# Folding the first channel mixer as well, with unread products in its pairs

## The chip, the cores and the metric

The kernel runs on one core of a Trainium2 chip. The metric is the device time of one execution in microseconds (us); lower is better. A run of the kernel is timed several times and the median is taken. The profile is one execution more, recorded by the hardware profiler.

## The reference

The reference is a decoder trunk of two layers over one sequence: T = 512 positions, D = 1024 channels, all in float32. Each layer is a token mixer and then a channel mixer, each behind an RMS norm that is modulated by a vector c (adaLN). Layer 0 has a retention as its token mixer, layer 1 an mLSTM. The channel mixer is the same in both layers:

```python
def conv_ffn(h, w_up, conv_w, conv_b, w_down):
    u = causal_dwconv(h @ w_up, conv_w, conv_b)
    a, b = jnp.split(u, 2, axis=-1)
    return (jax.nn.silu(a) * b) @ w_down

def reference(x, c, positions, ...):
    c_act = jax.nn.silu(c)
    for i in range(DEPTH):
        mod = c_act @ ada_w[i] + ada_b[i]
        sh_t, sc_t, gt_t, sh_f, sc_f, gt_f = [m[:, None, :] for m in jnp.split(mod, 6, axis=-1)]
        h = rmsnorm(x, norm_tok_g[i]) * (1.0 + sc_t) + sh_t
        ...
        x = x + gt_t * y
        h = rmsnorm(x, norm_ffn_g[i]) * (1.0 + sc_f) + sh_f
        x = x + gt_f * conv_ffn(h, ffn_w_up[i], ffn_conv_w[i], ffn_conv_b[i], ffn_w_down[i])
    return rmsnorm(x, final_g)
```

The hidden width is 2816, which is 22 tiles of 128 for each of the two halves a and b. "A pair" is the tile f of a and the tile f of b.

## The kernel before

**Products.** Every float32 operand is split into a high part that TensorE takes in one pass and a low part, the rest; a product is three matmuls, high x high, low x high and high x low (mm3, lines 250 to 253). A weight chunk is 128 x 1024 (512 KB): SyncE's queue (SP) loads it into one of 8 raw buffers, ScalarE (ACT) casts the high part (L157, whi) and VectorE (DVE) subtracts for the low part (L162, wlo).

**The program** is a list of items, and an item has the weight chunks that it uses. The loop at its end (lines 1363 to 1371) runs the items in order, and before each item it loads and splits chunks for up to 4 items ahead (class Ahead, line 331), as long as the 8 buffers for split weights allow and no "bar" is passed. `bars` holds the item at which a folded channel mixer starts; no chunk from behind a bar is fetched ahead of it.

**Side gemvs.** The vector c is multiplied with the adaLN weights on DVE: one gemv (line 130) takes a 512 KB load on SP's queue, into the same raw buffers, and one DVE instruction of 1025 elements a partition (L134). Those that aren't wanted at once stand in the list `side`, 80 of them, and one is taken from it after each item that uses weight chunks and is marked free:

```python
        fn([u.chunk for u in uses])
        if uses and free and n > 6 and side:
            side.pop(0)()
```

**The order of the stages** is: retention, channel mixer 0, mLSTM, channel mixer 1, with a seam between each two. At a seam (`boundary`, line 580) the last contraction of a stage is done in two halves of 256 positions, so that the norm of the first half (sums of squares, tile pms; DVE reciprocal; scaling) runs beside the products of the second, and the next stage's first four projections (tile pf, `Start.rest`, line 655) are done in halves too. In the mLSTM the items of `heads` (line 827) stand in this order: projections q, k of heads 0 and 1 with the scores of head 0 after the second projection of head 1, attend of head 0, values of head 1, and so on. The scores (`ml_scores`, line 1270) load two rows from a scratch in DRAM by SP's queue (mb, db), weigh the products with w = exp(...) (L1280 and L1281), and split the result (sp, sl); attend (tile pav) multiplies them with the values.

**Channel mixer 0** is direct: for each pair two projections with products of 512 columns (tile pp, 24 products each), the causal convolution over positions on ACT and DVE, silu and gate; after groups of 6, 8 and 8 tiles come the contractions with w_down (tile po).

**Channel mixer 1** is folded from pair 5 on (`FOLD_FROM`, 17 pairs). `Start.sums` (line 684) and `Start.turn` (line 707) form sums and differences of halves of the input; class Fold (line 183) forms the like of the weights, on DVE, ACT and GpSimd (POOL); seven products of 256 columns take the place of eight (`folded`, line 374; tile p, lines 387 to 389). A pair's products stand in `unit` (line 406) in the order 1, 5, 2, 6, first half of a contraction, 7, second half of it, 4, 3. On TensorE, DVE, ACT and POOL the fold runs in the order written. Its groups are 4, 4, 4, 4 and 6 tiles, and the contractions of the first four stand within the units. Ahead of the fold, items for the pairs 2 to 4 take in the first steps of the fold in pieces (`early`, in `Ffn.items`, line 945).

Of the kernel before, what the change touches and what calls it, by code (L numbers as in the profile page):

```python
# [22 lines left out]
FF = 2816  # L23
FT = FF // P
EPS = 1e-6
GROUPS = [[6, 8, 8], [4, 4, 4, 4, 6]]
WCOLS = 1024
WBUFS = 8
RAWS = 8
FOLD_FROM = 5  # L30
WPAD = 64
OFF = 16
DIRECT = (0, 0)
# [36 lines left out]
def trunk(ctx: ExitStack, tc: tile.TileContext, xT, cb, pos, vec, decay, zmask, ada, w_s0, w_in0, w_v0,  # L70
# [300 lines left out]
            then(ps)  # L371
        item([Use(src, KT * P)], fn)

    def folded(folds, h, terms, pairs, downs, ahead):

        no = lambda *a: None
        banks, sums = {}, {}

        def product(i, n, o, start=False):
            hi, hc, lo, lc = folds[i].p[n]
            for k in range(4):
                b = terms(n, k)
                st, sp = start and k == 0, n in (2, 3, 4) and k == 3
                ch, cl = slice(hc + k * P, hc + k * P + P), slice(lc + k * P, lc + k * P + P)
                PE.matmul(o, hi[:, ch], b[0], start=st, stop=False, skip_group_check=True)  # L387
                PE.matmul(o, hi[:, ch], b[1], start=False, stop=False, skip_group_check=True)  # L388
                PE.matmul(o, lo[:, cl], b[0], start=False, stop=sp, skip_group_check=True)  # L389
# [12 lines left out]
        def last(i):  # L402
            c1, s = banks[i][0], sums[i][0]
            V.tensor_tensor(c1[:, HB], c1[:, HB], s[:, HB], op=ALU.add)

        def unit(i):
            f = folds[i + 1] if i + 1 < len(folds) else None
            d = chunks[i + 1] if i + 1 < len(downs) else None
            with_down = i < len(downs)
            at = pairs[i - 1] if i else None  # L410
            if at:
                last(i - 1)
                at.init(1, banks[i - 1][1])
# [24 lines left out]
            if at:  # L438
                at.silu()
            V.tensor_tensor(c1[:, HA], c1[:, HA], s[:, HA], op=ALU.add)  # L440
            if at:
                at.gate()
            product(i, 6, c2[:, HA])
            A.copy(s[:, HB], c2[:, HA])
            if f:
                f.low_13()
                f.sums_24()
            else:
                ahead.low()
                ahead.low()  # L450
            if at:
                at.high()
                at.low()
            if with_down:
                down(i, 0)
            else:
                product(i, 5, c1[:, HB])
            if f:
                f.high_24()
                f.low_24(i % 2)  # L460
            else:
                ahead.high()
                ahead.high()
            product(i, 7, c2[:, HA])
            A.copy(q[:, HA], c2[:, HA])
            V.tensor_tensor(c2[:, HB], c1[:, HB], q[:, HA], op=ALU.add)
            if d:
                d.high()
                d.low()
            down(i, 1)  # L470
            if f:
                f.high_b()
                f.low_b()
            else:
                ahead.low()
                ahead.low()
            product(i, 4, c2[:, HA])
            product(i, 3, c1[:, HB])
            if i + 2 < len(folds):
                folds[i + 2].load()  # L480
            load_down(i + 2)
            if i == len(folds) - 2:
                for _ in range(4):
                    ahead.load()

# [375 lines left out]
    def gate_col(layer, which):  # L861
        base = (16, 40)[which]
        return lambda m: mods[layer][:, base + m : base + m + 1]


    class Ffn:
        def __init__(self, layer):
            self.layer, self.h, self.gs = layer, [], {}
            t0, t1 = self.pair(0), self.pair(1)
            w = w_up[layer]  # L870
            self.folded = layer == 1
            self.start = Start([w[0], w[FT], w[1], w[FT + 1]], self.h, layer, 1, [t0, t0, t1, t1], self.folded)

        def conv_col(self, f, j):
            return col("fcw", (self.layer * 3 + j) * 2 * FT + f)
# [62 lines left out]
                between()  # L938

        def down(self, gi):  # L940
            base = sum(GROUPS[self.layer][:gi])
            return pieces(lambda i: w_dn[self.layer][gi][i], GROUPS[self.layer][gi], gate_col(self.layer, 1),
                          lambda k: self.gs[base + k])

        def items(self, norm):
            groups = GROUPS[self.layer]
            if self.folded:
                w = w_up[self.layer]
                folds = [Fold((w[f], w[f + FT])) for f in range(FOLD_FROM, FT)]
                pairs = [self.steps(f) for f in range(FOLD_FROM, FT)]  # L950
                downs = [p for gi in range(len(groups) - 1) for p in self.down(gi)]
                steps, run = folded(folds, self.h, self.start.terms, pairs, downs, ahead)

                def early(n):
                    todo = [steps.pop(0) for _ in range(n)]
                    item([], lambda w: [f() for f in todo])
                self.up(2)
                early(1)
                self.up(3, lambda: early(3))
                th = self.pair(4)  # L960
                proj_item(w[4], self.h, th)
                early(len(steps))
                proj_item(w[4 + FT], self.h, lambda ps: (self.start.turn(), th(ps)))
                bars.append(len(items))
                item([], run)
                boundary([], self.down(len(groups) - 1), norm)
                return
            base, nxt = 0, 2
            for gi, n in enumerate(groups):
                upto = base + n + 2 if gi < len(groups) - 2 else FT  # L970
                while nxt < min(upto, FT):
                    self.up(nxt)
                    nxt += 1
                if gi < len(groups) - 1:
                    contract_items(self.down(gi))
                else:
                    boundary([], self.down(gi), norm)
                base += n


    cos, sin = slot("cos"), slot("sin")
# [381 lines left out]
    for n, (uses, fn, free) in enumerate(items):  # L1363
# [112 lines left out]
```

## Time and profile before

| | |
|---|---|
| median of 3 runs | 1569.84 us (1569.71 to 1570.32) |
| the profiled execution, own time | 1570.65 us |
| its span | 1568.8 us |
| mean granted TensorE clock | 0.993 |
| mixer 0, first whole-width product to last contraction | 456.55 to 795.80 us |
| mixer 1, the same | 1234.70 to 1557.60 us |

A row of the timeline gives start, duration, engine, line, operation, output<-input, sizes and count; in brackets stands how long the engine had been idle before it, and what released it. A record of a matmul lasts longer than its share of the stream, since matmuls overlap: the pace is read from start to start. PE is the matmul stream of TensorE, PEld its weight loads, which run beside it.

### The profile page before, as it was taken

The page shows a single profiled execution, that of the slowest core. Times are in us where ns is not written, and L with a number is a line of the kernel's source. Part 1 is how long each engine was busy: PE and PEld are TensorE (multiplying, and loading weights), DVE is VectorE, ACT ScalarE, POOL GpSimd, SP SyncE. Part 2 cuts the span into 40 slices and gives each one's busy share as a digit, 9 for nine tenths or more (in the row PEclk, how much of TensorE's full clock was granted, in tenths as well). Part 3 has the DMA queues.
Part 4 walks back from the last instruction along what each step waited for, and adds up shares of the span by engine and source line. Part 5 has one row for each costly group of instructions (what it writes and reads, how often), then busy time and mean ns, then how long its engine had stood idle before and what let it go on. Part 6 is the DMA issues. An engine that isn't in the chain of part 4 may idle for free. (4 is left out here: it accounts for less than half of the span.)

```text
span 1568.8 us, 21573 instructions
## 1 busy us (share of the span) xinstructions
PE 1539.3 (98%) x8428; PEld 1336.7 (85%) x8428; DVE 1136.2 (72%) x1631; ACT 772.1 (49%) x1142; POOL 186.2 (12%) x195
## 2 busy tenths in 40 slices
PE   7999999999999999999999999999999999999997
PEld 4788888888988888888998888888889889999997
DVE  7986678576979778764476667756588977777775
ACT  4534525353454334442356554555444666666763
POOL 3421010100200000000020011001022211111102
PEclk8999999999999999999999999999999999999999
DMA  8664365453236666533124322232312257767751
GB/s 297 223 198 135 101 228 181 162 181 119 97 97 197 225 207 188 174 102 99 55 86 133 105 74 75 94 107 68 107 54 74 76 132 203 175 189 187 184 140 54
DMA packets 66024, 219.14 MB, mean 140 GB/s; under 512 B 9073, under 2 KB 11377, under 8 KB 65922
## 3 DMA queue, kind: packets, MB, share of 16 engines
q1 hardware_dynamic: 59730, 195.22, 37.9%
q0 software_dynamic: 6192, 22.55, 7.7%
q8 instruction: 66, 1.08, 0.3%
q14 instruction: 36, 0.29, 0.1%
HBM read 193.06 MB, written 2.12 MB: 124 GB/s over the span
## 5 line engine op out<-in xcount | busy, mean ns | idle before, releaser
L162 DVE TENSOR_TENSOR wlo<-raw,whi 128x1024 fp32r<-128x1024 f32 (+1 forms) x224 | 271.5, 1214 | 135.2 <-ACT whi L157 133.8
L157 ACT CAST whi<-raw 128x1024 fp32r<-128x1024 f32 (+1 forms) x224 | 230.7, 1033 | 259.7 <-PE pp L252 95.9
L251 PE MATMUL pp<-hh,whi 128*128 128x512 f32 x832 | 323.9, 389 | 0.5 <-DVE vl L248 0.5
L252 PE MATMUL pp<-hl,whi 128*128 128x512 f32 x832 | 323.8, 389 | 0.0
L253 PE MATMUL pp<-hh,wlo 128*128 128x512 f32 x832 | 323.7, 389 | 0.0
L251 PEld LDWEIGHTS pp<-hh,whi 128*128 128x128 f32 x832 | 156.2, 188 | 33.4 <-DVE vl L248 1.0
L253 PEld LDWEIGHTS pp<-hh,wlo 128*128 128x128 f32 x832 | 156.2, 188 | 32.3
L252 PEld LDWEIGHTS pp<-hl,whi 128*128 128x128 f32 x832 | 156.2, 188 | 32.0
L550 DVE SCALAR_TENSOR_TENSOR x<-po,mod,x 128x512 f32<-128x512 f32 (+1 forms) x168 | 102.5, 618 | 95.8 <-PE po L253 95.7
L252 PE MATMUL po<-ggl,whi 128*128 128x512 f32 (+1 forms) x464 | 156.2, 337 | 0.0
L251 PE MATMUL po<-ggh,whi 128*128 128x512 f32 (+1 forms) x464 | 155.7, 337 | 0.1
L253 PE MATMUL po<-ggh,wlo 128*128 128x512 f32 (+1 forms) x464 | 155.8, 336 | 0.0
L252 PE MATMUL po<-yl,whi 128*128 128x256 f32 (+1 forms) x352 | 116.3, 330 | 0.0
L251 PE MATMUL po<-yh,whi 128*128 128x256 f32 (+1 forms) x352 | 116.2, 330 | 0.0
L253 PE MATMUL po<-yh,wlo 128*128 128x256 f32 (+1 forms) x352 | 116.2, 330 | 0.0
L134 DVE SCALAR_TENSOR_TENSOR ada<-ada,c_ext 128x1025 f32<-128x1025 f32 x93 | 114.9, 1239 | 0.0
L253 PEld LDWEIGHTS po<-ggh,wlo 128*128 128x128 f32 x464 | 87.1, 188 | 9.6
L251 PEld LDWEIGHTS po<-ggh,whi 128*128 128x128 f32 x464 | 87.1, 188 | 8.9 <-ACT ggh L913 0.3
L252 PEld LDWEIGHTS po<-ggl,whi 128*128 128x128 f32 x464 | 87.6, 189 | 8.2
L538 PE MATMUL pv<-wlo,hh 128*128 128x512 f32 x224 | 87.2, 389 | 0.0
L539 PE MATMUL pv<-whi,hl 128*128 128x512 f32 x224 | 87.0, 389 | 0.0
L537 PE MATMUL pv<-whi,hh 128*128 128x512 f32 x224 | 87.0, 389 | 0.0
(282 smaller groups left out, 3202.4 us busy)
## 6 DMA issues: line engine op xcount, KB each, us to landing
ada<-ada SPq DMA_DIRECT2D x96, 512.5 KB, 4.4
raw<-w_in SPq DMA_DIRECT2D x62, 512.0 KB, 3.4
raw<-w_up SPq DMA_DIRECT2D x54, 512.0 KB, 4.1
raw<-w_o SPq DMA_DIRECT2D x32, 512.0 KB, 3.3
raw<-w_dn SPq DMA_DIRECT2D x32, 512.0 KB, 4.4
raw<-w_v SPq DMA_DIRECT2D x28, 512.0 KB, 3.8
wb<-w_up SPq DMA_DIRECT2D x17, 512.0 KB, 3.8
wa<-w_up SPq DMA_DIRECT2D x17, 512.0 KB, 4.3
```

The lines of the kernel that those rows point to most:

```text
L134: return V.scalar_tensor_tensor(raw, raw, 1.0, c_ext[:], op0=ALU.mult, op1=ALU.mult, accum_out=mods[layer][:, f : f + 1])
L157: A.copy(hi, w[:, r])
L162: V.tensor_tensor(lo, w[:, r], hi.bitcast(F32), op=ALU.subtract)
L251: PE.matmul(o, ah, bh, start=start, stop=False)
L252: PE.matmul(o, ah, bl, start=False, stop=False)
L253: PE.matmul(o, al, bh, start=False, stop=stop)
L537: PE.matmul(pss[t][:], h[k].hi[:, cs], w[0].hi[:, ws], start=st, stop=False)
L538: PE.matmul(pss[t][:], h[k].hi[:, cs], w[0].lo[:, ws], start=False, stop=False)
L539: PE.matmul(pss[t][:], h[k].lo[:, cs], w[0].hi[:, ws], start=False, stop=sp)
L550: V.scalar_tensor_tensor(x[m][:, r], ps[:, r], gate_col, x[m][:, r], op0=ALU.mult, op1=ALU.add)
```

## The change

Both layers use the groups 4, 4, 4, 4, 6 and the folded mixer. `folded` gets an argument `extra`, true for layer 0: before the product with index 4 of pair i, for the first 16 pairs, the products in `EXTRA[i]` are done into a bank of their own (tile pd), which nobody reads. An entry (own, n) is one product of n columns, with 128 columns of the weights of that product 4 (own = 1) or of the contraction's chunk (own = 0). There are 19 of them, with n from 16 to 512, and two of the 16 lists are empty.

The side gemvs stop when 32 of them are left, until the items are past the first fold (`bars[0]`); then they go on, so that 32 which stood in mixer 0 come to stand in the mLSTM stage. In the order of instructions TensorE gets 581 more in all, DVE 151, ACT 140 and POOL 47, and SP has as many as before.

```diff
-GROUPS = [[6, 8, 8], [4, 4, 4, 4, 6]]
+GROUPS = [4, 4, 4, 4, 6]
 WCOLS = 1024
 WBUFS = 8
 RAWS = 8
+LATER = 32
 FOLD_FROM = 5
+
+EXTRA = [[], [(1, 32)], [(1, 64)], [(1, 128)], [(1, 192)], [(1, 256)], [(0, 32)], [(0, 64)], [(0, 128)],
+         [(1, 64)] * 2, [(1, 64)] * 4, [], [(1, 96)], [(1, 512)], [(1, 16)], [(1, 128)] * 2]
...
-    def folded(folds, h, terms, pairs, downs, ahead):
+    def folded(folds, h, terms, pairs, downs, ahead, extra):
...
                 ahead.low()
                 ahead.low()
+            if extra and i < len(EXTRA):
+                hi, _, _, _ = folds[i].p[4]
+                o = bank("pd") if EXTRA[i] else None
+                for own, n in EXTRA[i]:
+                    wt = hi[:, :P] if own else chunks[i].hi[:, :P]
+                    PE.matmul(o[:, :n], wt, h[0].hi[:, :n], start=True, stop=True)
             product(i, 4, c2[:, HA])
             product(i, 3, c1[:, HB])
...
-            self.folded = layer == 1
-            self.start = Start([w[0], w[FT], w[1], w[FT + 1]], self.h, layer, 1, [t0, t0, t1, t1], self.folded)
+            self.start = Start([w[0], w[FT], w[1], w[FT + 1]], self.h, layer, 1, [t0, t0, t1, t1], True)
...
         def items(self, norm):
-            groups = GROUPS[self.layer]
-            if self.folded:
-                w = w_up[self.layer]
-                folds = [Fold((w[f], w[f + FT])) for f in range(FOLD_FROM, FT)]
...
-                steps, run = folded(folds, self.h, self.start.terms, pairs, downs, ahead)
...
-            base, nxt = 0, 2
-            for gi, n in enumerate(groups):
-                upto = base + n + 2 if gi < len(groups) - 2 else FT
-                while nxt < min(upto, FT):
-                    self.up(nxt)
-                    nxt += 1
-                if gi < len(groups) - 1:
-                    contract_items(self.down(gi))
-                else:
-                    boundary([], self.down(gi), norm)
-                base += n
+            w = w_up[self.layer]
+            folds = [Fold((w[f], w[f + FT])) for f in range(FOLD_FROM, FT)]
+            pairs = [self.steps(f) for f in range(FOLD_FROM, FT)]
+            downs = [p for gi in range(len(GROUPS) - 1) for p in self.down(gi)]
+            steps, run = folded(folds, self.h, self.start.terms, pairs, downs, ahead, self.layer == 0)
...
+            bars.append(len(items))
+            item([], run)
+            boundary([], self.down(len(GROUPS) - 1), norm)
...
         fn([u.chunk for u in uses])
-        if uses and free and n > 6 and side:
+        if uses and free and n > 6 and side and (n > bars[0] or len(side) > LATER):
             side.pop(0)()
```

More of the change, by code (lines that the diff above doesn't have):

```diff
@@ L940, in down @@
         def down(self, gi):
-            base = sum(GROUPS[self.layer][:gi])
-            return pieces(lambda i: w_dn[self.layer][gi][i], GROUPS[self.layer][gi], gate_col(self.layer, 1),
+            base = sum(GROUPS[:gi])
+            return pieces(lambda i: w_dn[self.layer][gi][i], GROUPS[gi], gate_col(self.layer, 1),
                           lambda k: self.gs[base + k])
         def items(self, norm):
-            groups = GROUPS[self.layer]
-            if self.folded:
-                w = w_up[self.layer]
-                folds = [Fold((w[f], w[f + FT])) for f in range(FOLD_FROM, FT)]
-                pairs = [self.steps(f) for f in range(FOLD_FROM, FT)]
-                downs = [p for gi in range(len(groups) - 1) for p in self.down(gi)]
-                steps, run = folded(folds, self.h, self.start.terms, pairs, downs, ahead)
[L954 to L967, printed above, removed]
@@ new lines, in items, with early @@
+            pairs = [self.steps(f) for f in range(FOLD_FROM, FT)]
+            downs = [p for gi in range(len(GROUPS) - 1) for p in self.down(gi)]
+            steps, run = folded(folds, self.h, self.start.terms, pairs, downs, ahead, self.layer == 0)
+            def early(n):
+                todo = [steps.pop(0) for _ in range(n)]
+                item([], lambda w: [f() for f in todo])
+            self.up(2)
+            early(1)
+            self.up(3, lambda: early(3))
+            th = self.pair(4)
@@ L981, in trunk @@
+            proj_item(w[4], self.h, th)
+            early(len(steps))
+            proj_item(w[4 + FT], self.h, lambda ps: (self.start.turn(), th(ps)))
+            bars.append(len(items))
+            item([], run)
+            boundary([], self.down(len(GROUPS) - 1), norm)
     cos, sin = slot("cos"), slot("sin")
@@ L1463 @@
     for i in range(2):
-        for g, part in enumerate(_downs(a["ffn_w_down"][i], GROUPS[i])):
+        for g, part in enumerate(_downs(a["ffn_w_down"][i], GROUPS)):
             arrays[f"w_dn{i}{g}"] = c(part)
@@ L1471 @@
     with tile.TileContext(nc) as tc:
-        trunk(tc, *[args[n] for n in _ORDER], [[args[f"w_dn{i}{g}"] for g in range(len(GROUPS[i]))] for i in range(2)], out)
+        trunk(tc, *[args[n] for n in _ORDER], [[args[f"w_dn{i}{g}"] for g in range(len(GROUPS))] for i in range(2)], out)
     r = _run(nc, [arrays], core_ids=[0])
```

## The prediction

> **What bounds the kernel now.** I read the engine line of the page first, then the chain of waits, then the waits of TensorE, and last a table by stage.
>
> ```profile
> PE 1539.3 (98%) x8428; PEld 1336.7 (85%) x8428; DVE 1136.2 (72%) x1631; ACT 772.1 (49%) x1142; POOL 186.2 (12%) x195
> PE pf L252 <- DVE hl L308: 4.0, 4, 1.3
> PE pms L256 <- ACT ssh L247: 2.7, 2, 1.5
> ```
>
> TensorE (PE) is busy for 98% of the span, and its waits are few (engine, tile, line, releaser: total us, times, longest). The first two rows on them are the seams between a norm and the products behind it, 6.7 us together. So two things move the time: how long the stream of products is, and new holes in it. What VectorE (DVE) does counts only where PE runs into it.
>
> The two channel mixers compute the same thing with other weights, so the trace of before already holds the folded form. In the table by stretch (start:end, length, busy time and instructions of PE, weight load, DVE, ACT, POOL, granted clock, DMA share, GB/s) the first two rows run from the first whole-width product of a mixer to its last contraction, mixer 0 and mixer 1:
>
> ```profile
> 456.55:795.80 339.25, 339.25 (x1685) 288.79 (x1684) 238.15 (x329) 137.85 (x185) 8.71 (x8) 1.00 0.49 156
> 1234.70:1557.60 322.90, 322.78 (x2249) 301.07 (x2248) 240.99 (x369) 215.18 (x311) 43.23 (x51) 1.00 0.62 155
> 1322.28 0.28 PE L387 MATMUL p<-t3h,whi 128*128 128x256 f32 x1
> 1323.57 0.28 PE L389 MATMUL p<-t3h,wlo 128*128 128x256 f32 x1
> L252 PE MATMUL pp<-hl,whi x217: 389/389/389, 559.7 to 706.6; 128*128 128x512 f32 x109
> ```
>
> PE has no hole in mixer 0 and 0.12 us of holes in mixer 1. The third and fourth row are the first and the twelfth of a run of 256-wide products: 1.29 us over 11 steps, 0.1173 us from start to start, and 0.1178 over longer runs. The fifth row gives the 512-wide pace: 146.9 us over 216 steps of three products each, 0.2267 us a product.
>
> **Term 1, the fold and the new groups of mixer 0: -16.35.** It is the difference of the two stretches, 322.90 - 339.25, since after the change mixer 0 has the groups, the 17 folded pairs and the order of mixer 1. A check from the paces: a pair costs 48 products 512 wide directly (48 x 0.2267 = 10.88 us) and 84 products 256 wide folded (84 x 0.1178 = 9.90), 0.99 less, times 17 pairs is -16.8; the few tenths that are missing are contractions in another shape. The fold's extra work on DVE, ACT and POOL is in the second row too, and PE went through it there. The Trainium skill ("TensorE: Matmul & The Clock Gate", section "Back-to-back issue gap") gives N/2.4 + 2.5 ns, 215.8 and 109.2 ns for the two widths, by which the 17 pairs would save 20.2 us instead of 16.8 and the time would be 3.4 us lower, 1561.0, as an estimate of that page. The rows are of the same shapes in this very kernel and differ from it, so I give that case no chance of its own.
>
> **Term 2, the products that nobody reads: +2.4 (1.1 to 6.8).** There are 19 of them in 14 of the first 16 pairs of mixer 0: 17 narrower than 256, one of 256, one of 512. They stand between the contraction and the product with index 4, and in mixer 1 that place is covered by nothing: PE goes through without a hole, so each costs its whole pace. They write a bank of their own; each waits for nothing but the previous one, over a hundred products back, so no wait comes with them. No product narrower than 256 is in the trace. The cheapest price is by columns: from the two paces, (0.2267 - 0.1178)/256 = 0.00043 us a column and 0.009 fixed, over 2,160 columns and 19 products 1.1 us. What speaks against it is the weight load:
>
> ```profile
> L251 PEld LDWEIGHTS pp<-hh,whi 128*128 128x128 f32 x832 | 156.2, 188 | 33.4 <-DVE vl L248 1.0
> 1558.05 0.60 PE L289 MATMUL pms<-sq,ones_d 128*128 128x256 f32 x2
> L289 PE MATMUL pms<-sq,ones_d x4: 377/380/483, 1558.1 to 1559.3; 128*128 128x256 f32 x4
> ```
>
> Every product has a weight load of 128 columns, 188 ns in the record, and that doesn't shrink with the product. In the 256-wide runs loads and products follow each other at 0.118 us, so if the load sets the floor, each narrow product costs up to 0.118 as well: 18 x 0.118 + 0.227 = 2.35 us. The dearest price is that of the only products of this kernel in plain float32 (the two last rows): 0.38 us each on record, 17 x 0.38 + 0.118 + 0.227 = 6.8. I take 2.4, since each of them has that load. The Trainium skill says in the same page, section "LDWEIGHTS (loading the stationary operand)", that a load takes its columns over 1.2 GHz, whatever the product behind it; 107 ns for each would make term 2 2.2 instead of 1.1 us. No run so far shows a narrow product.
>
> **Term 3, the opening of mixer 0's fold: +1.4 (0 to 3.2).** Ahead of a fold stand sums of the input, low parts of the turned input (turn) and the first chunks' sums, on DVE, ACT and POOL. In mixer 1:
>
> ```profile
> 1224.00:1267.50 43.50, 43.50 (x239) 37.91 (x238) 37.90 (x65) 27.74 (x43) 4.70 (x6) 1.00 0.37 97
> 1266.79 0.42 DVE L248 TENSOR_TENSOR hl<-xr,hh 128x256 fp32r<-128x256 f32 x1 [0.39 <-ACT hh L247]
> 1267.59 0.28 PE L387 MATMUL p<-hh,whi 128*128 128x256 f32 x1
> L134 DVE SCALAR_TENSOR_TENSOR ada<-ada,c_ext 128x1025 f32<-128x1025 f32 x93 | 114.9, 1239 | 0.0
> ```
>
> The turned low parts are ready at 1267.21, 0.4 us before the fold starts at 1267.59 and 0.4 + 12 x 0.118 = 1.8 before its second product, the first that reads them. In mixer 0 four side gemvs (the rows of adaLN, 1.24 us each on DVE, last row) stay in the items of pair 2 and up to the limit, 4 x 1.24 = 5.0 us on top of 37.90 of 43.50. What is left free is 0.6 us, and the idle pieces are waits on ACT that can't all be filled. If all 5.0 reach the end of the queue, PE waits 5.0 - 1.8 = 3.2; if the idle pieces take them, nothing. I take some two thirds of the 5.0, 3.2 us, as late: 3.2 - 1.8 = 1.4.
>
> **Term 4, the seam from mixer 0 to the mLSTM: +3.1 (0 to 3.9).** The last group goes from 8 tiles to 6.
>
> ```profile
> 778.79 0.28 PE L256 MATMUL pms<-ssh,ones_d 128*128 128x256 f32 x1
> 800.47 0.43 DVE L248 TENSOR_TENSOR ssl<-ssq,ssh 128x256 fp32r<-128x256 f32 x1 [0.47 <-ACT ssh L247]
> 801.65 0.28 PE L256 MATMUL pms<-ssh,ones_d 128*128 128x256 f32 x1
> ```
>
> Between the two sums of squares (pms) PE has 22.86 us of products: 144 of contractions and 48 of the next projection. DVE works through residual adds, norms and weight parts meanwhile and has the last operand (ssl) at 800.90, 0.75 before PE wants it. With 6 tiles instead of 8, PE has 144 x 2/8 = 36 products fewer (4.24 us): 18.6 us. DVE has as many operations as before, for they go by output tile or by weight chunk of the projection behind the seam. It takes them until 800.90, 22.1 us. So pms waits 22.1 - 18.6 = 3.5, less some 0.4 that DVE itself idled there: 3.1. A hole of this length may also cost clock:
>
> ```profile
> 40.19 0.50 PE L1143 MATMUL pst<-whi,hl 128*128 128x512 f32 x1 [1.82 <-DVE hl L308]
> 42.41 0.63 PE L1143 MATMUL pst<-whi,hl 128*128 128x512 f32 x1
> 42.84 0.63 PE L1141 MATMUL pst<-whi,hh 128*128 128x512 f32 x1
> 44.12 0.47 PE L251 MATMUL pst<-hh,whi 128*128 128x512 f32 x1
> 1215.63 0.38 PE L256 MATMUL pms<-ssh,ones_d 128*128 128x256 f32 x1 [1.55 <-ACT ssh L247]
> ```
>
> After a hole of 1.82 us the products ran at 0.43 us from start to start (42.41 to 42.84), until 44.12; seven of them at 0.43 instead of 0.2267 are a loss of 1.4; after 1.55 us at 1215 they did not. Here the seam has another wait of 1.3 behind it (pf, first fence) that such a loss would only take the place of, so I add nothing. By the Trainium skill (same page, section "What's actually happening") the clock halves after an idle window of some 3.4 us; the trace shows it after 1.82 us already. By the page's figure no clock would be lost here, by the row up to 1.4; the sum is the same.
>
> **Term 5, the 32 side gemvs that move into the mLSTM stage: +4.0 (0 to 9).** From mixer 0 they only lift DVE load; PE had no hole there, so nothing is gained. In the mLSTM one follows each of the first 32 items with a weight chunk: 32 x 1.24 = 40 us of DVE, each behind a load of its own on SP's queue (third row below: 512.5 KB, 4.4 us to landing) into the same 8 raw buffers that the weights use.
>
> ```profile
> 832.00:900.00 68.00, 68.00 (x311) 56.72 (x310) 44.62 (x57) 35.23 (x51) 2.03 (x4) 1.00 0.38 110
> 100.00:120.00 20.00, 20.00 (x97) 16.98 (x96) 17.14 (x24) 5.62 (x9) 5.62 (x7) 1.00 0.51 164
> ada<-ada SPq DMA_DIRECT2D x96, 512.5 KB, 4.4
> 882.56 0.37 SPq L1273 DMA_DIRECT2D mb<-scratch  x1
> 887.42 0.35 DVE L1280 SCALAR_TENSOR_TENSOR w<-mb,bcols,zm 128x128 f32<-128x128 f32 x1 [0.26 <-DMA mb<-scratch]
> 889.54 0.69 DVE L1284 SCALAR_TENSOR_TENSOR sp<-psc,w 128x512 f32<-128x512 f32 x1 [1.77 <-ACT w L1281]
> 891.63 0.68 DVE L248 TENSOR_TENSOR sl<-sp,sh 128x512 fp32r<-128x512 f32 x1
> 894.58 0.39 PE L251 MATMUL pav<-sh,vh 128*128 128x512 f32 x1
> ```
>
> In 832 to 900 some 12.5 of them come to DVE: 44.62 + 12.5 x 1.24 = 60.1 of 68 us, 88%. The retention shows the same load (second row: 86% on DVE with a gemv to each chunk), and PE is unbroken there. So the projections themselves hold. The place at risk is the first head's scores: the weighing (w) waits for mb, which stands on SP behind the loads of raw buffers, and w heads a chain that lets attend (pav) start at 894.58. That chain has some 2.3 us to spare: the low part of the first scores is ready at 892.3. With loads coming later, up to one item's conversion (5.4 us, 24 products of 0.2267), and DVE's queue fuller, I put w at 893 to 898, 5.6 to 10.6 late, which makes a hole of 3.3 to 8.3, to 9 with clock. Between 0, as in the retention, for whose attend the list of TensorE's waits has no row, and the middle of the later band (5.8) I take 4.0, nearer to the band, since mb has no counterpart in the retention. Later heads come when most of the 32 are gone, and I count nothing there.
>
> **The sum** against the profiled execution's 1570.65 us: -16.35 + 2.4 + 1.4 + 3.1 + 4.0 = -5.45, 1565.2. The median lies 0.81 below that execution, so 1564.4 on its scale. The measurement can tell 0.2% (3.1 us) from no change.
>
> **The rivals.** *Holes filled* (terms 3 and 5 at nothing): -16.35 + 2.4 + 3.1 = -10.85, 1559.0 by the median. For it: the retention row, and mixer 1's opening without a hole. Against it: the short slack in both places. With term 2 at its low end too it is 1557.7. *Scores starved*, the slower side: each of the last conversions before the first scores waits a whole turn of the ring of raw buffers (5.4 to 5.7 us), w comes at about 906, the hole at attend is 14.6 instead of 4.0: -5.45 + 10.6 = +5.2, 1575.0. It decides from a w later than 902. Against it: the ring is 8 deep and loads are issued four items ahead. *Narrow products dear*, at 0.38 us each: +4.4 on the forecast, 1568.8. *Unread products at no cost*, because product 4 waits for a low part anyway and they fall into that wait: -2.4, 1562.0; mixer 1's PE row, without holes, speaks against it.
>
> **How the numbers follow.** Forecast 0.45 (own range 1561 to 1567.5), holes filled 0.27, unread at no cost 0.04, narrow dear 0.12, scores starved 0.12. Faster by over 0.2% is under 1566.7: four fifths of the forecast, all of the filled holes and of the free products, a little of the dear ones, 0.36 + 0.27 + 0.04 + 0.01 = 0.68. Slower is above 1573.0: 0.10 of the starved case, and 0.01 of the dear one, 0.11; the rest, 0.21, is no change. For the range I take 1556.5 (filled holes, with the unread products and the seam at lower prices) to 1572.5 (dear products and a long hole), which leaves out the starved case and a small part of the other end.
>
> **What would show it.** In the profile after: mixer 0's stretch near 323 us plus term 2, with pace 0.118; the unread products' start-to-start times by width, flat at 0.11 to 0.12 if the weight load sets them, growing with columns if not, 0.2 or more if the form is dear; a hole of some 3 us at the pms of the seam to the mLSTM; w of the first scores at some 6 to 10 us later against its projections, and a hole before pav. It is wrong if mixer 0's stretch has holes within its units, or if pav starts late by over 10 us.

## The result: slower by 1.0%

The changed kernel takes 1585.57 us (1584.51 to 1586.88, 4 runs) against 1570.08 of the kernel before, a ratio of 1.0099 with a 95% interval of 1.0082 to 1.0117. It is 15.5 us slower, where 5.5 us of gain were forecast, and lies above the range. The direction was wrong.

The page of the changed kernel (busy time of the engines) and its list of TensorE's waits (tile, line, releaser: total us, times, longest):

```profile
PE 1530.5 (97%) x9011; PEld 1352.4 (85%) x9011; DVE 1201.4 (76%) x1782; ACT 859.7 (54%) x1282; POOL 227.8 (14%) x242
PE pav L255 <- ACT sh L251: 8.2, 1, 8.2
PE pms L260 <- ACT ssh L251: 4.5, 3, 1.8
PE pp L255 <- DVE vl L252: 4.1, 2, 3.0
PE p L393 <- DMA wlo<-wt: 2.7, 1, 2.7
PE p L391 <- ACT fs L428: 2.2, 1, 2.2
```

TensorE (PE) is busy for 8.8 us less than before, although the kernel is longer: what came on top is waiting. Before, the two longest waits behind those of the start were the seams. Now, behind the start, attend of the mLSTM's first head (pav) heads the list, and one wait of 3.0 in the mLSTM (pp) and two at the start of mixer 0's fold (p) are new on it.

The table by stretch, for both kernels between the same marks: where the products of 512 columns set in behind a seam, where the seam's first projection starts, and so on. In the changed kernel all marks are set 0.40 us ahead of these events, which leaves the lengths as they are. The first five rows are the kernel before, the next five the changed kernel: mixer 0, the projections of the seam, the mLSTM, the second seam, mixer 1. The columns are length, busy time of PE, weight load, DVE, ACT, POOL, granted clock, DMA share, GB/s:

```profile
456.74:795.99 339.25, 339.25 (x1684) 288.79 (x1683) 238.34 (x329) 137.85 (x185) 8.71 (x8) 1.00 0.49 156
795.99:819.95 23.96, 22.66 (x196) 22.47 (x195) 14.53 (x25) 9.01 (x18) 3.38 (x4) 1.00 0.18 60
819.95:1208.26 388.31, 387.59 (x1924) 329.54 (x1923) 263.74 (x354) 198.87 (x294) 40.31 (x44) 1.00 0.29 89
1208.26:1234.92 26.66, 23.71 (x196) 23.07 (x195) 25.87 (x47) 10.98 (x24) 7.74 (x9) 1.00 0.11 40
1234.92:1557.81 322.89, 322.77 (x2248) 301.06 (x2247) 240.77 (x368) 215.18 (x311) 43.23 (x51) 1.00 0.62 155
```

```profile
456.74:788.83 332.09, 325.57 (x2267) 302.64 (x2267) 253.96 (x387) 221.33 (x317) 45.01 (x51) 0.99 0.68 173
788.83:815.85 27.02, 23.75 (x196) 22.96 (x195) 19.04 (x33) 10.95 (x24) 3.48 (x5) 1.00 0.26 86
815.85:1223.19 407.34, 392.85 (x1924) 332.42 (x1924) 301.50 (x427) 200.20 (x294) 41.97 (x43) 0.98 0.40 127
1223.19:1249.44 26.25, 23.27 (x196) 22.63 (x195) 25.50 (x45) 10.98 (x24) 8.15 (x10) 1.00 0.14 42
1249.44:1572.28 322.84, 322.72 (x2248) 301.02 (x2248) 241.41 (x370) 215.23 (x311) 43.11 (x51) 1.00 0.62 155
```

Mixer 0 gained 7.2 us instead of 12.6 (terms 1 to 3), the seam lost 3.1, and the mLSTM lost 19.0 with the same 1924 products. Everything before 456.74 and behind 1223.19 is as it was, within half a us. So two places hold most of the loss: the mLSTM and the first 20 us of the fold. In the mLSTM 13.8 of the 19.0 us are more waiting (14.5 against 0.7) and 5.3 are the same products taking longer (392.85 against 387.59), at a mean clock of 0.98.

Where the fold begins, the timeline of the changed kernel shows two long holes with two products between them, then products at half clock (0.43 us from start to start for a contraction's 512 columns, against 0.229 later; the granted clock is 0.50 from 499.8 to 506.6):

```profile
498.16 0.39 PE L391 MATMUL p<-t24h,whi 128*128 128x256 f32 x1 [2.16 <-ACT fs L428]
501.35 0.58 PE L393 MATMUL p<-t24h,wlo 128*128 128x256 f32 x1 [2.68 <-DMA wlo<-wt]
...
503.85 0.43 PE po L255
504.28 0.43 PE po L256
```

The last two rows are from the chain of waits (start, length, step). Holes and clock together are some 9 us of the mixer's 332.

### The profile page after: what moved, and what is told of

Its sections match the earlier page's. It is cut to its first block, busy times and chain, and to the rows that moved or that the text cites. A ratio compares the mean times of both kernels' runs of the same rounds, so it can differ in the third digit from the quotient of the medians.

```text
span 1583.7 us, 23100 instructions
## 1 busy us (share of the span) xinstructions
PE 1530.5 (97%) x9011; PEld 1352.4 (85%) x9011; DVE 1201.4 (76%) x1782; ACT 859.7 (54%) x1282; POOL 227.8 (14%) x242
## 4 chain that ended last, share of the span: by engine, by line
PE 77%; DVE 14%; ACT 4%; DMA 2%; issue 2%; POOL 0%; SPq 0%; DVEq 0%; ACTq 0%; POOLq 0%
PE po L255 8%; PE po L256 8%; PE po L257 8%; PE p L391 7%; PE p L393 7%; PE p L392 7%; PE pp L255 6%; PE pp L256 6%; PE pp L257 6%; PE pv L549 3%; PE pv L548 3%; PE pv L547 3%; DVE wlo L166 3%; DVE ada L138 2%; DVE hl L312 1%
## 5 line engine op out<-in xcount | busy, mean ns | idle before, releaser
L255 PE MATMUL pp<-hh,whi 128*128 128x512 f32 x560 | 218.9, 391 | 4.1 <-DVE vl L252 4.1
L256 PE MATMUL pp<-hl,whi 128*128 128x512 f32 x560 | 218.6, 390 | 0.0
L257 PE MATMUL pp<-hh,wlo 128*128 128x512 f32 x560 | 218.4, 390 | 0.0
L391 PE MATMUL p<-hh,whi 128*128 128x256 f32 x544 | 152.2, 280 | 0.7 <-ACT hh L251 0.7
L392 PE MATMUL p<-hl,whi 128*128 128x256 f32 x544 | 152.2, 280 | 0.6 <-DVE hl L252 0.6
L393 PE MATMUL p<-hh,wlo 128*128 128x256 f32 x544 | 152.1, 280 | 0.0
L255 PEld LDWEIGHTS pp<-hh,whi 128*128 128x128 f32 x560 | 105.4, 188 | 26.4 <-DVE vl L252 4.8
L888 ACT ACTIVATE cv<-p,vecs 128x512 f32<-128x512 f32 x68 | 53.0, 780 | 115.8 <-PE p L393 78.1
L392 PEld LDWEIGHTS p<-hl,whi 128*128 128x128 f32 x544 | 103.4, 190 | 0.8 <-DVE hl L252 0.8
L391 PEld LDWEIGHTS p<-hh,whi 128*128 128x128 f32 x544 | 102.4, 188 | 1.0 <-ACT hh L251 0.9
```

The source lines that it names most:

```text
L255: PE.matmul(o, ah, bh, start=start, stop=False)
L256: PE.matmul(o, ah, bl, start=False, stop=False)
L257: PE.matmul(o, al, bh, start=False, stop=stop)
L888: A.activation(acc[:], ps[:], AF.Identity, bias=col("fcb", self.layer * 2 * FT + f), scale=self.conv_col(f, 2))
```

## The experiments

Times of a kernel are compared with runs of the kernel before on the same chip.

**Without the unread products.** `EXTRA = [[]] * 16`.

> The changed kernel without the 19 unread products; everything else as in the changed kernel. Theory A (a short product costs almost nothing, and the run of 256-wide products behind it goes at 0.1133 us instead of 0.1178): all units of mixer 0 take 15.39 us again, so the fold is 0.6 us longer than with them and the time 0.3 to 1.0 us above the changed kernel's. Theory B (the prediction's price, 2.4 us, hidden in the holes of the profile): 2.0 to 2.5 us below the changed kernel.

1585.23 us, ratio 1.0098 (1.0083 to 1.0113), against 1.0099 for the changed kernel: no difference that can be told, and the intervals are too wide for the 0.6 us of theory A. The traces decide. In mixer 0 TensorE is busy for 325.5 us without the unread products and for 325.6 with them, so the price of 2.4 us is not there. The other half of it shows in the changed kernel's trace. Below are two of its runs of 72 products behind an unread one, grouped by operands (min, median, max of the durations in ns, first and last start). The first row is behind a product of 32 columns with the fold's weights, the second behind one of 64 columns with the contraction's weights:

```profile
L391 PE MATMUL p<-hh,whi x16: 276/276/276, 528.8 to 533.9; 128*128 128x256 f32 x16
L391 PE MATMUL p<-hh,whi x16: 281/281/281, 620.7 to 626.0; 128*128 128x256 f32 x16
527.34 0.18 PE L486 MATMUL pd<-hh,whi 128*128 128x32 f32 x1
527.37 0.37 PE L391 MATMUL p<-t24h,whi 128*128 128x256 f32 x1
527.57 0.28 PE L392 MATMUL p<-t24l,whi 128*128 128x256 f32 x1
```

Each of the sixteen is every third product, so 45 steps take 5.1 and 5.3 us: 0.1133 and 0.1178 us a product. The last three rows are the start of the first run: the unread product takes 0.03 us, the one behind it 0.20, together 0.23, which is about 0.11 more than one product of 0.118. The 72 products behind give back 0.32.

**The opening's four gemvs earlier.** Four items at the retention's end take two each.

```diff
+            for _ in range(2 if n in (53, 54, 55, 56) else 1):
+                side.pop(0)()
-            side.pop(0)()
```

> The changed kernel with the four side gemvs of mixer 0's opening done earlier: four items of the last head's projections in the retention take two each. Theory A (the opening's holes, some 10 us from 491 to 507, come from DVE, which these four keep back, so that sums, low parts and the adding load of the last low part start late): nearly all holes there go, 7 to 10 us below the changed kernel. Theory B (the chain of loads, sums and adding loads of the fold's first pair is itself too long after 25 us of opening, gemvs or not): under 3 us gained.

1579.75 us, 1.0058 (1.0043 to 1.0073): 5.8 us below the changed kernel, between the two theories. The same 21 us of the opening in the table by stretch, first the changed kernel, then this one:

```profile
487.00:508.00 21.00, 14.88 (x76) 12.68 (x75) 12.42 (x23) 13.17 (x20) 2.56 (x3) 0.84 0.83 197
487.00:508.00 21.00, 18.40 (x109) 15.77 (x108) 15.73 (x26) 13.00 (x22) 1.70 (x2) 1.00 0.32 67
```

The adding load is a load that adds what it brings to a low part that ScalarE has begun (wlo<-wt). The wait for it and the half clock behind it are gone, a wait of 1.5 for the sum of the fold (fs) remains. Mixer 0 is 5.6 us shorter (326.5 against 332.1). Four gemvs of 1.2 us on DVE cost 5.8 us: their delay passes through a chain of casts and loads, and half clock follows the holes.

**The mLSTM's gemvs without their work, or without their loads.** In the first kernel the 32 gemvs multiply 8 columns (their adaLN values are left out), in the second they multiply a resident tile in two instructions of 512 columns and load nothing (the values are left out as well).

```diff
# load only
+        nc.sync.dma_start(raw, ada[layer, f])
+        V.scalar_tensor_tensor(raw[:, :8], raw[:, :8], 1.0, c_ext[:, :8], ...)
# work only
+        for h in range(2):
+            V.scalar_tensor_tensor(late[0][:], late[0][:], 1.0, c_ext[:, h * T : h * T + T], ...)
```

> The changed kernel, but the 32 side gemvs of the mLSTM stage multiply 8 columns instead of 1025 (their adaLN values are left out): the loads and the raw buffers stay, 32 x 1.2 us of DVE goes. Theory A (the ring of 8 raw buffers, shared with the weights, sets the holes at 891 to 905 and 1044): the hole before attend of head 0 stays over 5 us and the time falls by less than 6 us. Theory B (DVE's queue sets them): hole under 2 us, 13 to 19 us below the changed kernel.

> The changed kernel, but the 32 side gemvs of the mLSTM stage multiply a resident tile (two instructions of 512 columns, as long as one of 1025) and load nothing: DVE's work stays, the loads and raw buffers go. Theory A (ring of raw buffers): hole before attend of head 0 under 2 us, 12 us or more below the changed kernel. Theory B (DVE's queue): hole over 5 us, less than 6 us below it.

With the loads alone 1569.62 us, 0.9996 (0.9986 to 1.0005): 16 us are back, the wait on pav is down to 1.0 us and that on pp is gone. With the work alone 1581.51 us, 1.0073 (1.0056 to 1.0090): 4 us are back, and these stay:

```profile
PE pp L262 <- DVE vl L259: 5.0, 1, 5.0
PE pav L262 <- ACT sh L258: 4.4, 1, 4.4
```

So DVE's queue makes most of the loss, and the loads with the ring of raw buffers add some 4 us to it. DVE before the first scores in the changed kernel (timeline; idle time before an operation and its releaser in brackets), and at the end the first product behind each of the mLSTM's two long holes:

```profile
884.73 1.23 DVE L138 SCALAR_TENSOR_TENSOR ada<-ada,c_ext 128x1025 f32<-128x1025 f32 x1 [0.89 <-DMA ada<-ada]
...
886.48 1.22 DVE L138 SCALAR_TENSOR_TENSOR ada<-ada,c_ext 128x1025 f32<-128x1025 f32 x1
...
893.17 1.23 DVE L166 TENSOR_TENSOR wlo<-raw,whi 128x1024 fp32r<-128x1024 f32 x1 [2.23 <-ACT whi L161]
894.32 0.68 DVE L252 TENSOR_TENSOR mqkl<-mc,mqkh 128x512 fp32r<-128x512 f32 x1
894.92 1.22 DVE L138 SCALAR_TENSOR_TENSOR ada<-ada,c_ext 128x1025 f32<-128x1025 f32 x1
896.27 1.23 DVE L166 TENSOR_TENSOR wlo<-raw,whi 128x1024 fp32r<-128x1024 f32 x1
897.41 0.35 DVE L1275 SCALAR_TENSOR_TENSOR w<-mb,bcols,zm 128x128 f32<-128x128 f32 x1
...
899.79 0.80 PE L255 MATMUL pav<-sh,vh 128*128 128x512 f32 x1 [8.21 <-ACT sh L251]
...
1045.21 0.50 PE L255 MATMUL pp<-hh,whi 128*128 128x512 f32 x1 [3.03 <-DVE vl L252]
```

The gemvs stand between the parts that the next products and the scores need; each in turn waits for its load, and DVE takes its work in order. w comes at 897.41 and attend starts at 899.79 after a hole of 8.2. By then 13 of the 32 gemvs have run; the last one starts at 1031. In the 68 us that answer to the prediction's 832 to 900 (828.3 to 896.3 here) DVE had 9 gemvs and was busy for 50.9 us, 75%: it was not overloaded, it was late.

**The 32 gemvs on GpSimd and ScalarE.** `gemv_pool(layer, f, raw)` in place of the DVE instruction, for the mLSTM's 32; then that and the four earlier gemvs together, without and with one short product in all 34 pairs.

> The changed kernel, with the 32 side gemvs of the mLSTM stage on GpSimd (multiply) and ScalarE (sum) instead of DVE; loads and buffers as they are. Theory A (DVE's queue makes the holes): most of the 16 us of the kernel with the shortened gemvs come back, 8 to 15 below the changed kernel, less what POOL's small operations ahead of attend and the group norms wait. Theory B (any engine in that chain does it): under 4 us.

> Both repairs together (four gemvs earlier in the retention, 32 on GpSimd and ScalarE) and no unread products. Sum of the parts: 1585.6 + 0.3 - 5.8 - (8 to 15) = 1565 to 1572, faster than the kernel before if the mLSTM's holes go.

> The same with one unread product of 64 columns, with the weights of the next product, in each of the 34 pairs of both mixers. Theory A (0.1133 behind a short product with the next product's weights): 34 x 0.19 = 6.5 us below the kernel without them, 1559 to 1566. Theory B (each costs a pace of 0.118, and nothing comes back): 4 us above it.

1603.44 us (1.0207, 1.0192 to 1.0222), 1595.66 (1.0160, 1.0145 to 1.0175) and 1591.87 (1.0133, 1.0116 to 1.0150). All three missed. DVE is relieved, but other engines of the chain make TensorE wait. From the groups of GpSimd and TensorE's waits in the first of them:

```profile
L142 POOL TENSOR_TENSOR ada<-ada,c_ext 128x1025 f32<-128x1025 f32 x30 | 77.6, 2589 | 120.4 <-DMA ada<-ada 76.3 <-ACT mc L1265 11.1 <-DVE gain L161 10.4
PE pvar L266 <- DVE vl L258: 4.2, 1, 4.2
PE psc L261 <- ACT mqkh L257: 4.0, 1, 4.0
```

A multiply takes 2.6 us there, and ScalarE, which sums it in order, holds the casts of the projections (mqkh) behind it; that this is why is read from these rows, not tried by itself. The third kernel is 3.8 us below the second: 34 short products save time, less than the 6.5 expected.

**One kind of unread product a pair.**

> The changed kernel with other unread products, one kind a pair, in both mixers, for the trace. Mixer 0: one product of 64 columns with the weights of the next product in all 16 first pairs but pair 8, which has the contraction's weights. Mixer 1, pairs 0 to 16: contraction's weights x64, none, contraction's weights x64, two own x64 (twice), own x256, own x224, own x240, three own x64 (twice), contraction's weights x512 (twice), own x384, weights of the low part x64, weights of product 3 x64, own x512, own x64. Theory A (a short product with the weights of the next product lets the 72 products behind it go at 0.1133): all of mixer 0's pairs but the eighth go at 0.1133 and take 15.19 us, all with other weights 0.1178 and 15.50. Theory B (it was the position in the stream, which happened to be the same for those pairs): paces mixed within the uniform pairs of mixer 0.

1582.97 us, one execution. All sixteen pairs of mixer 0 behave as theory A says, but the rule is wider. The table has this kernel's pairs and those of the changed kernel; the pair is the time from one unread product to the next pair's:

| unread product before product 4 | pace of the 72 behind it | pair |
|---|---|---|
| one, 16 to 384 columns but not 256, weights of the fold (the next product's; at 64 columns also those of the low part or of product 3) | 0.1133 | 15.18 to 15.26 |
| one of 512, weights of the fold | 0.1133 | 15.31 (changed kernel) |
| three or four of 64, weights of the fold | 0.1133 | 15.41, 15.53 (four: changed kernel) |
| two of 64, or one of 256, weights of the fold | 0.1178 | 15.61, 15.51 |
| one of 32 to 128, or of 512, weights of the contraction | 0.1178 | 15.50, 15.61 |
| none | 0.1178 | 15.39 |

So it is not the weights of the next product, as theory A had it, but those of the fold. These lie at column 16 of their buffers (`OFF`), the contraction's at column 0. Two of 128, the changed kernel's last list, give 0.1133 too. Why two of 64 or one of 256 columns change nothing stays open.

**The contraction's weights at column 16.**

```diff
-                chunks[i].__init__(u.src, u.n, 0)
+                chunks[i].__init__(u.src, u.n, OFF)
```

> The changed kernel without unread products, and with the contraction's weight chunks of the folds put 16 columns into their buffers, as the fold's own weights are (before: at column 0). Theory A (what holds the 256-wide products at 0.1178 is the step from weights at column 0 to weights at column 16, so that a short product helped only with weights at column 16): the runs of 256-wide products go at 0.1133 without any short product, a pair takes 15.0 to 15.1 us, 34 pairs are 10 to 13 us shorter than in the kernel without unread products. Theory B (a product of another length is needed, wherever the weights lie): pairs of 15.39 as before, no change against the kernel without unread products; the 512-wide contractions may get slower.

1581.01 us, 1.0070 (1.0055 to 1.0084): 4.2 us below the kernel without unread products. The 256-wide products go at 0.1134 in every pair of both mixers, with no short product. The exception is the opening: the first 36 of a fold, in mixer 1 without a hole, stand behind projections with weights at column 0 and go at 0.1178. The contraction pays for it: the rows are every third of 12 of its products in this kernel, then in the changed one; the 12 go from start to start at 0.2329 and 0.2288 us on average.

```profile
L255 PE MATMUL po<-ggl,whi x4: 393/396/399, 569.3 to 571.4; 128*128 128x512 f32 x4
L256 PE MATMUL po<-ggl,whi x4: 389/391/397, 524.8 to 526.9; 128*128 128x512 f32 x4
```

A pair takes 84 x 0.1134 + 24 x 0.2329 = 15.11 us, 0.28 less than the 15.39, which for 34 pairs is some 9.4 us. Only 4.2 came out against the kernel without unread products. By the traces the two mixers are 7.6 us shorter together (328.2 and 319.2 against 331.8 and 323.3), but the mLSTM is 4.5 us longer (411.0 against 406.5): tile pden waits 3.4 us for ACT here and 0.9 in the kernel without unread products, and 6.8 us at half clock come with it. Why this wait grew was not looked into; in a chain with such holes a time saved ahead of them can be lost again.

**Other places for the mLSTM's gemvs.** A table says after which items a gemv is taken: none beside the projections of q and k and the values of heads 1 to 3, one or two beside gate projections, contractions and the values of head 0.

```diff
+PLACES = {n: 1 for n in (126, 127, 128, 129, 147, 148, 149, 150, 152, 153, 154, 155, 167, 168, 169, 170,
+                         187, 189, 191, 192, 194, 195)} | {n: 2 for n in (125, 182, 183, 184, 185)}
-        if uses and free and n > 6 and side and (n > bars[0] or len(side) > LATER):
-            side.pop(0)()
+        if uses and free and side and (n > 6 and len(side) > LATER or n > bars[0] and n in PLACES):
+            for _ in range(PLACES.get(n, 1)):
+                side.pop(0)()
```

> The changed kernel with the 32 side gemvs of the mLSTM stage at other items: none beside the projections of q and k and the values of heads 1 to 3; one or two beside the gates' projections and the contractions. Theory A (it is DVE's queue ahead of the first scores and the first end that makes the holes): the hole before attend of head 0 under 1.5 us, that at the end of head 1 gone, 10 to 15 us below the changed kernel. Theory B (32 gemvs in this stage cost as much wherever they stand): under 5 us.

1566.89 us, 0.9981 (0.9972 to 0.9990): 18.7 us below the changed kernel, more than either theory gave. The same work and the same loads, at other items: the table by stretch over nearly the whole mLSTM,

```profile
815.00:1204.00 389.00, 387.28 (x1920) 329.06 (x1919) 299.78 (x427) 198.67 (x293) 41.45 (x43) 1.00 0.42 133
```

has DVE as busy as in the changed kernel (299.8 and 301.5) and PE without a product for 1.7 us instead of 14.5. Between the marks used above, the mLSTM takes 389.6 us, 1.3 more than in the kernel before.

**All of it.** The placed gemvs, the four earlier ones, and either a short product of 64 columns in each pair or the contraction's weights at column 16.

> Three repairs together: four gemvs earlier in the retention, the 32 placed as in the kernel with other items, and one unread product of 64 columns with weights of the fold in each of the 34 pairs. Sum of the parts: 1585.6 - 5.8 - (10 to 15) - 6 = 1559 to 1564, below the kernel before. If the holes only move, 1570 or more.

> The same placing, no unread products, and the contraction's chunks at column 16. By theory A on the weights' place 1552 to 1558, by theory B 1565 to 1570.

1557.26 us, 0.9919 (0.9905 to 0.9932), and 1552.94 us, 0.9891 (0.9877 to 0.9904). The first lies a little below the sum of its parts, the second where theory A put it. Both beat both kernels; the second is 32.6 us below the changed kernel and 16.8 below the kernel before in these runs. Its mixers:

```profile
455.48:776.92 321.44, 319.10 (x2249) 295.20 (x2248) 247.43 (x374) 221.81 (x317) 45.01 (x51) 1.00 0.69 175
1220.27:1539.05 318.78, 318.50 (x2249) 295.38 (x2248) 240.87 (x369) 216.89 (x311) 43.02 (x51) 1.00 0.63 157
```

Mixer 1, which both kernels fold, is 4.1 us shorter here than in the kernel before (322.89). That part of the 16.8 us comes from the place of the weights and not from folding mixer 0; the kernel before with column 16 alone was not run.

**The place of the weights.**

> The placed kernel without unread products, for the trace: the contraction's chunk of pair i lies at column 0, 4, 8, 12, 16, 20, 24, 28, 32, 40, 48, 56, 60, 64, 2, 1 of its buffer; the fold's weights lie at column 16 in mixer 0 and at 0 in mixer 1. Theory A1 (it counts whether chunk and fold lie at the same place modulo 16 columns, 64 bytes): mixer 0 at 0.1133 behind chunks at 16, 32, 48, 64 and 0 fails; in mixer 1 the fold is fast behind 0, 16, 32, 48, 64 alike. Theory A2 (column 0 of the fold's weights is slow for 256-wide products as such): mixer 1 at 0.1178 or more in all pairs. Theory A3 (any place of the chunk but 0 lets the fold go): mixer 0 at 0.1133 in all pairs but the first; the 512-wide contraction at 0.2288 at some of the places would then be the better choice.

1562.94 us, one execution. In mixer 1, with the fold's weights at column 0, the 72 products go at 0.1197 to 0.1200 behind all sixteen places: theory A2 holds for column 0. In mixer 0 (fold at 16) they go at 0.1134 to 0.1136 behind chunks at 2, 8, 12, 16, 32, 40, 48 and 56, and at 0.1178 behind 0, 1, 4, 20, 24, 28, 60 and 64, so neither A1 nor A3 holds. At 48 both were fast in that run: 0.2290 for the contraction, 0.1143 and 0.1136 for the fold. Each place stands behind one pair a mixer in one execution, and the next two kernels show that such a reading need not hold again.

**The contraction's weights at column 48,** in the best kernel and alone in the kernel before.

> The placed kernel with no unread products and the contraction's chunks of both folds at column 48. From the probe of places a pair takes 24 x 0.2290 + 12 x 0.1143 + 72 x 0.1136 = 15.05 us against 15.11 at column 16 and 15.39 at column 0: 34 pairs are 2 us below the kernel with column 16, 1550 to 1552. If the pace behind column 48 was of that one pair alone: 1553 or more.

> The kernel before with this one edit: the contraction's chunks in mixer 1's fold at column 48. If the place of the weights acts by itself, the 17 pairs take 15.05 us instead of 15.39, 4.9 to 5.8 us below the kernel before. If it needs the other changes: no change.

1558.55 us (1553.32 to 1566.12), 0.9929 (0.9909 to 0.9949), and 1572.26 us (1564.16 to 1573.02), 1.0004 (0.9992 to 1.0015): the gain came out in neither. The same layout has one pace or the other. In the profiled execution of the first, the whole of one mixer went at 0.2290 and 0.1135, the whole of the other at 0.2335 and 0.1178; in that of the second all pairs of mixer 1 went at 0.2335 and 0.1178. Two of ten executions of the second, at 1564.16 and 1564.94, came near the expected 1564, so the pace seems to change from one execution to the next as well; no trace of a fast one was taken. Column 16 gave 0.2329 and 0.1134 in every pair of the profiled executions of the two kernels that have it; their executions lie within 6.3 and 2.0 us of each other.

## Why the prediction was wrong, point by point

**Term 1** (-16.35, the fold of mixer 0) was right: mixer 0 without its holes and its half clock is as long as mixer 1, some 323 us (332.09 less 6.5 of waiting and 2.4 that its first products lost at half clock).

**Term 2** (+2.4, the unread products) was not there. The step that failed is that each costs its own pace and the rest goes on as it did. The two paces from which the price by columns was made were not fixed prices: 0.1178 was one of two paces of the same products. By pairs of the changed kernel, six that took 15.18 to 15.20 us and one of 15.31 save 0.2 and 0.1 each against 15.39, and six that took 15.50 to 15.61 lose 0.1 to 0.2: some 0.4 us saved together. That is luck of the mixture of widths and weights in the list, not a price. The floor of the weight load by the Trainium skill ("TensorE: Matmul & The Clock Gate", section "LDWEIGHTS (loading the stationary operand)"), 107 ns, is borne out where products of 64 columns follow each other: from the second on their starts lie 0.108 to 0.112 us apart. The first step, behind a contraction's product of 512 columns, is only 0.03. A single one takes 0.23 us together with the 256-wide product behind it.

**Term 3** (+1.4, at most 3.2; the opening) came out at some 9, of which the earlier gemvs gave back 5.8. The place, the cause (four gemvs, DVE) and the first products that wait were right. Wrong was the price: the delay was put only on the turned low parts. The chain behind it (sums on DVE, cast and negation on ACT, the adding load of 9.4 us, the next product) delays two further products by 2.2 and 2.7 us, and half clock followed these gaps, which was counted at the seam and not here. The prediction's own sign of being wrong, holes within the units of mixer 0, is this.

**Term 4** (+3.1, the seam) was right in size, 27.02 - 23.96 = 3.06 us between the stretches, but not in its make-up: waiting rose by 2.0 us only (27.02 - 23.75 against 23.96 - 22.66; the hole at pms is 1.8 and not 3.1), and the same 196 products were busy for 1.1 us longer, which was not forecast and whose cause is open. So the size was met in part by luck.

**Term 5** (+4.0, at most 9; the moved gemvs) came out at 19, and this is the largest miss. Place and first cause were named, with w late by 5.6 to 10.6 us. It came 13.7 late (897.41 against 887.42, in a stage that began 3.7 earlier, at 816.25 against 819.95), and the hole before attend, 8.2, lay within the forecast's band of 3.3 to 8.3. Four steps failed. The band was averaged with nothing to 4.0, because the retention was taken as the nearest row; but the mLSTM's DVE queue has other work between the projections. The hole was taken as the only one, since "most of the 32 are gone" when the later heads come. In the trace 13 had run when attend of head 0 began; smaller holes follow at the norms of the heads, and one of 3.0 (pp) where DVE still has the end of head 1 to do ahead of the values of head 2. The clock falls at the two long ones. And the load was judged by its mean, 88% of DVE where 75% was measured, though DVE waits within those 68 us for loads and casts; what is left free can't be used by work that stands in order behind a wait.

**The rivals.** "Scores starved" (1575.0, a chance of 0.12) was the nearest in place and sign, but its mechanism, a turn of the ring of raw buffers for each conversion, was the smaller part: taking the loads away gave back 4 us, taking DVE's work away 16. The hole was 8.2 and not 14.6, but it was not alone. "Unread products at no cost" was nearly true of the sum, but not for its reason: no wait hid them. The chance of 0.11 for slower was too small because terms 3 and 5 each had a ceiling made from one wait.

**The clock.** With holes of 2.68 (behind one of 2.16), 3.03 and 8.2 us came stretches of 6.8, 3.4 and 10.2 us at a granted clock of 0.5, as the prediction's rows of 1.82 had shown. The seam's 1.83 cost none, but in the kernel with the earlier gemvs the same hole (1.81) was followed by 3.4 us at 0.5. By the Trainium skill (same page, section "What's actually happening") the window is some 3.4 us and runs freely; that shorter holes than 3.4 are at times enough and at times not is what these rows show.

## What to carry to other kernels

Work that is moved off an engine's slack stage is priced by what stands behind it in that engine's order, not by the mean load: 32 gemvs cost 19 us at some items and 1.3 at others of the same stage. A hole in TensorE's stream is rarely alone; count the waits that the same delay meets further on, and the clock. And before a pace from a trace is used as a price, look whether the same instruction has another pace elsewhere: here 0.1178 and 0.1133 us for the same product, apart by where the weights of the products ahead of it lie in their buffers.

## What the runs showed of the hardware

A 256-wide product with weights at column 16 of its buffer goes at 0.1133 or 0.1178 us, for a whole run of up to 84 products. In every trace with these two places it went by what stood before: the contraction's weights at column 0 lead to 0.1178, at column 16 to 0.1134, and one short product with weights at column 16 changes it from the first to the second (one of 256 columns or two of 64 don't). With the fold's weights at column 0 it is 0.1197 to 0.1200. The contraction's 512-wide products go at 0.2288 with their weights at column 0 and 0.2329 at column 16. At column 48 the pace differs between the two mixers of one execution, and by the times also between executions, so the place alone does not decide there. Why it matters was not found, and no place was found that is fast for both widths each time.
